# Three moves in a hybrid decoder block: B's bonus, down's first split, and the PSUM pool of one run of small matmuls

## The chip, the cores and the metric

The kernel runs on one core of a Trainium2 chip. The metric is the device time of one execution in microseconds (us). A core has a matmul engine (TensorE, PE in the profile, with its weight loads shown as PEld), a vector engine (VectorE, DVE), a scalar engine (ScalarE, ACT), GpSimd (POOL), and a queue engine that issues most transfers (SyncE, SP). Each engine takes its own instructions in a fixed order and waits on semaphores for the others. Matmuls write into PSUM, of which the kernel has eight banks of 128 x 512 float32; DVE and ACT read results out of there.

## What is computed

The reference is one layer of a hybrid decoder over 16 meta tokens and 1024 tokens, width 1024:

```python
h = h + 0.5 * swiglu(rmsnorm(h), w_gu, w_down)             # first feed-forward network
aq, ak, av, az, abeta, aalpha, bcols, ga, gb = split(rmsnorm(h) @ w_in)
o_a = gated DeltaNet in chunks (aq, ak, av, ...)            # branch A, 8 heads of 128
o_b = RWKV-7 time mixing (bcols, ...)                       # branch B, 16 heads of 64
h = h + (sigmoid(ga) * o_a + sigmoid(gb) * o_b) @ w_out
h = h + 0.5 * swiglu(rmsnorm(h), w_gu2, w_down2)            # second network
return rmsnorm(h)
```

Two pieces of it are touched directly. Branch B adds a **bonus** to its output: `sum(r * k * r_k) * v`, the sum going over the 64 channels of a head. And the first matmul of the second half of each network (`down`) needs the hidden activations as its right-hand side.

## The kernel before

All large products are float32 products made of three matmuls on split operands: an operand x is written as hi + lo, where hi is a rounded copy (one ACT copy) and lo = x - hi (one DVE subtraction). The function `split` (L155) issues both, so in the profile ACT L159 is always a "hi" and DVE L160 a "lo". A weight tile of 128 x 1024 is loaded by SP (`wraw`), split into `w[:, 0]` and `w[:, 1]`, and used by 24 matmuls of 512 columns (`mm3`, L261): per 128 rows of the weight one with hi and hi, one with hi of the weight and lo of the activation, one with lo of the weight. At most one weight tile is split ahead of the one in use (`AHEAD`, `loadw`).

The time falls into three stages: the first network (to about 740 us), the middle with both branches (to about 2340 us), and the second network.

**The networks.** `gate_up` goes through the gate and up weights in units of seven half-size products each. Its hidden rows go to HBM (`hid`) and come back as `hr`, three loads ahead (`Hidden.AHEAD`); `Hidden.put` splits a row into an `hd` tile. The generator `Hidden.ahead` is stepped by the last two units of `gate_up`: its stages issue, in this order, the first loads, then nothing, a weight fetch, the first split into the tile `hd0`, nothing, a weight fetch. `down` then multiplies the rows by the down weights (`pd` in the profile).

**The middle.** It runs 16 passes, one for each of eight column groups (j) and two segments of the sequence. The first eight passes have 528 columns (512 and the meta tokens), the last eight 512. Each pass is a list of actions, each a function, and the actions of neighbouring passes are interleaved by hand: `REGULAR` is "merge_blocks transitions operands+ inverses+ chains gates finish decay++ new_b++ new_a++", where one + means the next pass and two the one after. So the order of the text around the change is: `transitions` of a pass, `operands` of the next; and `new_b`, then `new_a` of the one after.

- `new_b` (L1138) makes three projections (v, k, r), then the normalised key `kkn` by a column sum (`cs`), then by some nine DVE operations the tiles AR and BK, and at its end the bonus: `bv = r * r_k * k` (L1181), a split of `bv` into `hl`, two matmuls with a block-diagonal matrix of ones (`bon`, through `colsum`, L1032), and the multiplication by v (L1186).
- `new_a` (L1189) makes three projections, each followed by a convolution of three taps on DVE (L1209), a sigmoid on ACT, and, for the first two, a column sum (`cs`) through the same `hl` tile, of which there is one.
- `operands` makes the products `grb` (evacuated into LT, L1250), `gra` (evacuated into UA and attn, L1290 and L1292), `bkt`, `vp` and others, all in banks of the pool `mx`. LT and UA go to HBM and come back as `Ub`, which is the input of `inverses`: 62 small DVE operations (L1400, L1402), whose result goes through HBM again to `merge_blocks`.
- `transitions` (L1464) makes a serial row of small products by `run` (L1085): `xp`, `xp` again, `vp`, `mp` and at last `np`, each in two banks. Results of `mp` are read by six DVE operations (mt, L1508, four times; AR, L1511, twice), those of `np` by five (vbk, L1514 and L1515; yb, L1517).
- `chains` is the recurrence itself, 4 steps for A and 8 for B, each a matmul and a DVE or ACT operation in turn, in banks of the pool `ch`. `finish` ends the pass. The last pass has the order `FINAL`: "gates merge_blocks transitions chains fill finish", with half of the output projection (`pwo`) as `fill`.

The eight PSUM banks of the middle: the pool `ch` has two. The pool `mm` for projections has two tiles of two banks, and `mx` two banks, up to the action `banks` in the seventh pass; from there `mm` has three tiles of one bank and `mx` three. The small rotating tiles of DVE and ACT (xr, acc, v, k, r and others) share eight buffers (`NTMP`).

The framework records the instructions in the order of the text, gives each tile its buffer and each engine its order and its waits. The orders are fixed when the program is built, by a plan that takes an instruction as soon as it holds it to be ready.

Of the kernel before, what the change touches and what calls it, by code (L numbers as in the profile page):

```python
# [9 lines left out]
F32R = mybir.dt.float32r  # L10
AF = mybir.ActivationFunctionType
ALU = mybir.AluOpType
# [14 lines left out]
FULL = 512  # L27
# [127 lines left out]
def split(g, src, hi, lo, eng=None, hi_eng=None):  # L155
    if hi_eng:
        hi_eng.tensor_copy(hi, src)
    else:
        g.nc.scalar.activation(hi, src, AF.Copy)  # L159
    (eng or g.nc.vector).tensor_tensor(lo, src, hi.bitcast(F32), op=ALU.subtract)  # L160
# [400 lines left out]
class Hidden:  # L561
# [20 lines left out]
    def ahead(self):  # L582
        for f in range(self.AHEAD):
            self.load(f)
        yield
        yield
        fetchw(self.g)
        yield
        self.first = self.put(self.tile(self.pool, F32R, "hd0", "hd0", 1, [2]))
        yield  # L590
        yield
        fetchw(self.g)
        yield
# [330 lines left out]
def proj(g, c, ct, full=False):  # L924

    w = loadw(g, "win", ct)
    lo, n = (c.off, FULL) if full else (0, c.n)
    ps = mm_tile(g, "pp", n, FULL // 2 + c.off)
    for c0, cn in halves(n, FULL // 2 + c.off):
        sl = slice(lo + c0, lo + c0 + cn)  # L930
        mm3(g, ps[:, c0 : c0 + cn], w, KD, lambda k: (c.u[k][:, 0, sl], c.u[k][:, 1, sl]))
    return ps
# [135 lines left out]
def run(g, pool, name, *kinds):  # L1068


    ps, out, used = {}, [], [0, 0]
    for f in kinds:
        ds = [f(i, 0)[2] ^ f(i, 0)[3] for i in range(2)]
        at = []
        for d in ds:
            if d not in ps:
                ps[d] = pool.tile([P, 512], F32, name=name, tag=pool.name)
            at.append(used[d])
            used[d] += NCB // 2 * CB
        for i in range(NCB):  # L1080
            e, c0 = ds[i & 1], at[i & 1] + i // 2 * CB
            for h in range(2):
                l, r, src, dst = f(i, h)
                assert src ^ dst == e
                g.nc.tensor.matmul(ps[e][HS[dst], c0 : c0 + CB], lhsT=l, rhs=r, start=True, stop=True)  # L1085
        out.append([(ch3(ps[d][:, c0 : c0 + NCB // 2 * CB], CB), cs) for d, c0, cs in zip(ds, at, EO)])
    return out
# [50 lines left out]
def new_b(g, q):  # L1138

    nc, st, V, c, j, n, off, it = g.nc, g.st, g.V, q.c, q.j, q.n, q.off, q.it  # L1140
    meta = q.s == 0
    fs = slice(off, off + FULL)
    tmp = lambda name, w=528: tmp_tile(g, name, w)
    EN, ELx, av, elm = q.EN, q.ELx, q.av, meta and q.elm

    v = shifted(g, c, 48 + j, 16 + j, "vB")


    Vs = q.Vs = st.tile([P, NCB, CB], F32, name="Vs", tag="Vs", bufs=2)
    k = shifted(g, c, 40 + j, 8 + j, "kB")  # L1150
    for ps, cs in run(g, g.mx, "vbp", lambda i, h: (v[HS[h], off + i * CB : off + (i + 1) * CB],
                                                    g.C("cmat")[HS[h], HS[h]], h, key(i, h)))[0]:
        nc.scalar.activation(Vs[:, cs], ps, AF.Copy)
    if meta:
        ps = g.mx.tile([P, 512], F32, name="vbm", tag="mx")
        nc.tensor.matmul(ps[:16, 0:P], lhsT=v[:, 0:16], rhs=g.C("cmat"), start=True, stop=True)
        nc.scalar.activation(g.uvm[it % 2][0:16, :], ps[:16, 0:P], AF.Copy)

    r = shifted(g, c, 32 + j, j, "rB")
    kkn = tmp("kkn")  # L1160
    colsum_rsqrt(g, "bd", k[:, :n], kkn, kkn, n, 1.0, V("eps"), pre=V("kk", j))
    nc.vector.scalar_tensor_tensor(kkn[:, :n], k[:, :n], V("kk", j), kkn[:, :n], op0=ALU.mult, op1=ALU.mult)
    t1 = tmp("t1")
    nc.vector.tensor_tensor(t1[:, :n], av[:, :n], kkn[:, :n], op=ALU.mult)
    nc.scalar.activation(av[:, :n], av[:, :n], AF.Identity, scale=V("ka", j), bias=V("oka", j))
    nc.vector.tensor_tensor(k[:, :n], k[:, :n], av[:, :n], op=ALU.mult)
    BK = q.BK = st.tile([P, NCB, 2, CB], F32, name="BK", tag="BK")
    nc.vector.tensor_tensor(BK[:, :, 1, :], ch3(k[:, fs], CB), ch3(EN[:, fs], CB), op=ALU.mult)
    nc.vector.scalar_tensor_tensor(BK[:, :, 0, :], ch3(t1[:, fs], CB), -1.0, ch3(EN[:, fs], CB),
                                   op0=ALU.mult, op1=ALU.mult)  # L1170
    AR = q.AR = st.tile([P, NCB, 2, CB], F32, name="AR", tag="AR", bufs=2)
    nc.vector.tensor_tensor(AR[:, :, 0, :], ch3(kkn[:, fs], CB), ELx[:, :, 0:CB], op=ALU.mult)
    if meta:
        arm = q.arm = st.tile([P, 16], F32, name="arm", tag="arm", bufs=2)
        nc.vector.tensor_tensor(arm, kkn[:, 0:16], elm[:, 0:16], op=ALU.mult)
        nc.vector.tensor_tensor(g.bkm[:, 0:16], k[:, 0:16], EN[:, 0:16], op=ALU.mult)
        nc.vector.scalar_tensor_tensor(g.bkm[:, 32:48], t1[:, 0:16], -1.0, EN[:, 0:16], op0=ALU.mult, op1=ALU.mult)

    nc.vector.tensor_tensor(AR[:, :, 1, :], ch3(r[:, fs], CB), ELx[:, :, 1:], op=ALU.mult)
    bv = q.bv = st.tile([P, FULL], F32, name="bv", tag="bv", bufs=2)  # L1180
    nc.vector.scalar_tensor_tensor(bv, r[:, fs], V("rk", j), k[:, fs], op0=ALU.mult, op1=ALU.mult)  # L1181
    ps = g.mx.tile([P, 512], F32, name="bon", tag="mx")
    hi, lo = parts_tile(g, FULL)
    split(g, bv, hi, lo)
    colsum(g, ps, "bd", hi, lo)
    nc.vector.tensor_tensor(bv, ps, v[:, fs], op=ALU.mult)  # L1186


def new_a(g, q):  # L1189

    nc, st, V, c, j, n, off = g.nc, g.st, g.V, q.c, q.j, q.n, q.off
    meta = q.s == 0
    tmp = lambda name, w=528: tmp_tile(g, name, w)
    kq = q.kq = st.tile([P, 2, 528], F32, name="kq", tag="kq", bufs=2)
    for wi, base in ((0, 8), (1, 0), (2, 16)):
        ct = base + j
        ps = proj(g, c, ct)
        xr = tmp("xr", 531)
        acc = tmp("acc")
        if c.s == 0:  # L1200
            nc.gpsimd.memset(xr[:, 0:3], 0.0)
        else:
            nc.gpsimd.tensor_copy(xr[:, 0:3], g.carA[:, ct, :])
        nc.scalar.activation(xr[:, 3 : 3 + n], ps, AF.Copy)
        nc.scalar.activation(acc[:, :n], ps, AF.Identity, scale=V("convw", ct * 4 + 3))  # L1205
        if c.s == 0:
            nc.gpsimd.tensor_copy(g.carA[:, ct, :], xr[:, n : n + 3])
        for tap in (2, 1, 0):
            nc.vector.scalar_tensor_tensor(acc[:, :n], xr[:, tap : tap + n], V("convw", ct * 4 + tap), acc[:, :n],  # L1209
                                           op0=ALU.mult, op1=ALU.add)  # L1210
        sg = xr
        sigm(nc, sg[:, :n], acc[:, :n], scale=-1.0)
        nc.vector.tensor_tensor(acc[:, :n], acc[:, :n], sg[:, :n], op=ALU.mult)
        if wi < 2:
            colsum_rsqrt(g, "ones", acc[:, :n], sg, sg, n, 1.0, V("eps"),
                         bias=V("lnq") if wi == 1 else None)
            nc.vector.tensor_tensor(kq[:, wi, :n], acc[:, :n], sg[:, :n], op=ALU.mult)
    Va = q.Va = st.tile([P, NCA, P], F32, name="Va", tag="Va", bufs=2)
    ps = g.mx.tile([P, 512], F32, name="vap", tag="mx")
    for i in range(NCA):  # L1220
        nc.tensor.transpose(ps[:, i * P : (i + 1) * P], acc[:, off + i * CA : off + (i + 1) * CA], g.C("ident"))
    nc.scalar.activation(Va, ch3(ps, P), AF.Copy)
    if meta:
        vkm = q.vkm = st.tile([16, 2, P], F32, name="vkm", tag="vkm", bufs=2)
        ps = g.mx.tile([P, 512], F32, name="vmp", tag="mx")
        nc.tensor.matmul(ps[:16, 0:P], lhsT=acc[:, 0:16], rhs=g.C("ident"), start=True, stop=True)
        nc.scalar.activation(vkm[:, 0, :], ps[:16, 0:P], AF.Copy)
# [236 lines left out]
def transitions(g, q):  # L1464

    nc, st = g.nc, g.st
# [3 lines left out]
    xa, xv = (st.tile([P, NCB, CB], F32, name=x, tag=x) for x in ("xa", "xv"))  # L1470
# [9 lines left out]
    def by_tok(l, r):  # L1480
        def f(i, h):
            t = tok(i, h)
            return l(HS[t], i), r(HS[t], i), t, h
        return f
# [18 lines left out]
    bt = lambda r, i: BKt[r, i, i & 1]  # L1503
    br = lambda r, i: LT[r, i, i & 1, CB:]
# [4 lines left out]
                                    op=ALU.add)  # L1509
    for ps, cs in pr:  # L1510
        nc.vector.tensor_tensor(AR[:, cs, 1, :], ps, AR[:, cs, 1, :], op=ALU.add)  # L1511
    pn, py = run(g, g.ch, "np", by_tok(bt, lambda r, i: xv[r, i]), by_tok(lambda r, i: xv[r, i], br))
    for ps, cs in pn:
        nc.vector.tensor_tensor(vbk[:, cs], ps, vbk[:, cs], op=ALU.add)  # L1514
    nc.vector.tensor_tensor(vbk, vbk, q.gam.unsqueeze(2).to_broadcast([P, NCB, CB]), op=ALU.mult)  # L1515
# [222 lines left out]
```

## Time and profile before

| | us |
|---|---|
| median of 3 runs | 3052.4 |
| the runs | 3052.31 to 3053.04 |
| the profiled execution: its own time | 3048.16 |
| its span, first to last instruction | 3046.4 |
| PE busy, first network and its down (0 to 740) | 725.67 of 740 |
| PE busy, the middle (740 to 2340) | 1524.02 of 1600 |
| PE busy, second network (2340 to 3046) | 692.58 of 706 |
| DVE busy in the same three | 392.91, 1226.64, 388.19 |

The profile comes from one execution of its own, 4.2 us faster than the median of the runs. Its page gives each engine's busy time; the trace behind it gives every instruction with its start, and for an idle stretch ahead of it the instruction that ended the stretch (written `[idle <- what ended it]`). A row of the timeline reads: start, duration (us), engine, line, operation, output <- inputs, shape, how many in a row. A row of the waits reads: who waited <- for whom: total us, times, the longest. A row of the windows reads: the stretch, its length, then the busy time of PE, PEld, DVE, ACT and POOL with the number of instructions, the granted clock of PE as a share, the share of the transfer engines, and GB/s.

### The profile page before, as it was taken

Reading aid. Unit: us, or ns where it says so; the run is one execution under the profiler, and the core shown is the slowest. Engines: PE = TensorE matmul, PEld = TensorE weight load, DVE = VectorE, ACT = ScalarE, POOL = GpSimd, SP = SyncE. Lnnn points to the kernel's source line nnn. Section 1 sums busy time; section 2 is a strip of 40 time slices with the busy share of each in tenths; the row PEclk is TensorE's granted clock in tenths of the full one; section 3 lists DMA queues with packets and bytes.
Section 4 is the critical chain, followed back from the end, with each engine's and each line's share of the span. In section 5 each row is a group of like instructions: output and inputs, shape, how many; then the busy total and the mean of one; then the engine's idle time right before and its main releaser. Section 6 shows DMA issues by size and latency. Waiting matters only on the chain.

```text
span 3046.4 us, 61663 instructions
## 1 busy us (share of the span) xinstructions
PE 2942.3 (97%) x25498; PEld 2530.1 (83%) x25498; DVE 2007.7 (66%) x3872; ACT 1372.2 (45%) x2404; POOL 348.6 (11%) x503
## 2 busy tenths in 40 slices
PE   8999999999989999999998999999999999999998
PEld 8999998998878888888776777777786888888886
DVE  7555554346668877778868888777766755556246
ACT  5322222125645656556565655665544432223114
POOL 0322220000000000000000110010000032232000
PEclk9999999999999999999999999999999999999999
DMA  3232224234222322233332333223345132225223
GB/s 127 83 98 84 83 82 160 81 94 149 80 67 72 78 74 67 78 82 97 82 92 67 91 80 81 74 74 88 106 145 178 64 104 90 83 83 202 58 80 115
DMA packets 257593, 287.19 MB, mean 94 GB/s; under 512 B 169296, under 2 KB 175440, under 8 KB 257312
## 3 DMA queue, kind: packets, MB, share of 16 engines
q1 hardware_dynamic: 253072, 271.43, 30.2%
q0 software_dynamic: 2512, 8.65, 0.8%
q8 instruction: 201, 3.29, 0.5%
q10 hardware_dynamic: 1728, 3.16, 0.3%
q14 instruction: 80, 0.66, 0.1%
HBM read 232.70 MB, written 50.47 MB: 93 GB/s over the span
## 4 chain that ended last, share of the span: by engine, by line
PE 52%; DVE 10%; ACT 5%; issue 2%; DMA 1%; SPq 0%; DVEq 0%; ACTq 0%
PE pp L261 16%; PE pg L448 13%; PE pd L261 8%; PE pwo L261 3%; PE pg L472 1%; DVE w L160 1%; DVE tb L1400 1%; DVE Xb L1402 1%; ACT w L159 1%; PE vp L1085 1%; PE cs L1032 1%; PE mp L1085 1%; PE np L1085 1%; DVE mt L1508 1%; PE bkt L1317 1%
## 5 line engine op out<-in xcount | busy, mean ns | idle before, releaser
L261 PE MATMUL pp<-uk,w 128*128 128x512 f32 (+2 forms) x4824 | 966.6, 346 | 9.3 <-DVE w L160 5.7
L261 PEld LDWEIGHTS pp<-uk,w 128*128 128x128 f32 x4824 | 741.3, 190 | 105.5 <-DVE w L160 13.2
L159 ACT ACTIVATE w<-wraw 128x1024 fp32r<-128x1024 f32 (+2 forms) x330 | 326.4, 989 | 497.5 <-PE pd L261 301.7
L261 PE MATMUL pd<-hd,w 128*128 128x512 f32 (+2 forms) x2448 | 454.4, 346 | 5.3 <-ACT hd L159 3.1
L160 DVE TENSOR_TENSOR w<-wraw,w 128x1024 fp32r<-128x1024 f32 (+2 forms) x330 | 403.2, 1222 | 74.8 <-ACT w L159 64.9
L261 PEld LDWEIGHTS pd<-hd,w 128*128 128x128 f32 x2448 | 391.8, 189 | 63.9 <-ACT hd L159 3.3
L448 PE MATMUL pg<-bt,w 128*128 128x256 f32 (+2 forms) x2520 | 400.7, 317 | 0.0
L448 PEld LDWEIGHTS pg<-bt,w 128*128 128x128 f32 x2520 | 360.4, 188 | 32.8
L454 DVE TENSOR_TENSOR c<-c,pg 128x520 f32<-128x520 f32 (+1 forms) x280 | 189.6, 689 | 278.3 <-PE pg L448 250.6
L448 PE MATMUL pg<-b,w 128*128 128x256 f32 (+2 forms) x2160 | 347.8, 317 | 0.0
L448 PEld LDWEIGHTS pg<-b,w 128*128 128x128 f32 x2160 | 309.8, 188 | 28.0
L159 ACT ACTIVATE w<-wrx 128x1024 fp32r<-128x1024 f32 (+1 forms) x64 | 58.4, 913 | 289.8 <-PE pg L448 247.9
L418 POOL TENSOR_TENSOR wrx<-wrx 128x512 f32<-128x512 f32 x38 | 52.5, 1382 | 732.8 <-DVE w22b L160 519.0
L1402 DVE TENSOR_TENSOR Xb<-Xb,tb 115x126 f32<-115x126 f32 (+22 forms) x496 | 125.4, 253 | 9.1 <-DVE tb L1400 0.4
L1400 DVE TENSOR_TENSOR tb<-Ub,Xb 115x126 f32<-115x126 f32 (+22 forms) x496 | 124.1, 250 | 8.1 <-DMA Ub<-scr 0.9
L1209 DVE SCALAR_TENSOR_TENSOR acc<-xr,pk,acc 128x528 f32<-128x528 f32 (+1 forms) x144 | 108.8, 756 | 28.6 <-ACT acc L1205 28.0
L624 DVE SCALAR_TENSOR_TENSOR h<-pd,h 128x528 f32<-128x528 f32 (+1 forms) x64 | 44.6, 698 | 116.4 <-PE pd L261 116.4
L624 DVE SCALAR_TENSOR_TENSOR hh<-pd,hh 128x512 f32<-128x512 f32 x64 | 44.1, 690 | 115.2 <-PE pd L261 115.2
L261 PE MATMUL pwo<-uk,w 128*128 128x512 f32 x384 | 99.7, 413 | 4.1 <-DVE w L160 1.9
L261 PEld LDWEIGHTS pwo<-uk,w 128*128 128x128 f32 x384 | 73.8, 197 | 21.9 <-ACT w L159 2.7
L160 DVE TENSOR_TENSOR w<-wrx,w 128x1024 fp32r<-128x1024 f32 (+1 forms) x64 | 66.6, 1041 | 14.9 <-ACT w L159 14.8
L159 ACT ACTIVATE hd<-hr 128x1040 fp32r<-128x1040 f32 (+1 forms) x40 | 41.2, 1061 | 63.3 <-DMA hr<-hid 38.3
(420 smaller groups left out, 4200.4 us busy)
## 6 DMA issues: line engine op xcount, KB each, us to landing
wraw<-in_win SPq DMA_DIRECT2D x150, 512.0 KB
wraw<-in_wgu SPq DMA_DIRECT2D x44, 512.0 KB
wrx<-in_wgu SPq DMA_DIRECT2D x44, 512.0 KB
wraw<-in_wdn SPq DMA_DIRECT2D x48, 320.0 KB
wraw<-in_wdn SPq DMA_DIRECT2D x32, 384.0 KB
hid<-c SPq DMA_DIRECT2D x44, 260.0 KB
hr<-hid SPq DMA_DIRECT2D x22, 520.0 KB
hid<-c SPq DMA_DIRECT2D x44, 256.0 KB
```

Of the source, the lines that this page charges most:

```text
L159: g.nc.scalar.activation(hi, src, AF.Copy)
L160: (eng or g.nc.vector).tensor_tensor(lo, src, hi.bitcast(F32), op=ALU.subtract)
L261: g.nc.tensor.matmul(ps, lhsT=l, rhs=r, start=i == 0, stop=i == n - 1)
L418: sums.tensor_tensor(a22, a21, a22, op=ALU.add)
L448: nc.tensor.matmul(ps[:, c0 : c0 + cn], lhsT=l[:, x, k, :], rhs=r[:, k, y, c0 : c0 + cn], start=i == 0, stop=i == 3 * HK - 1)
L454: nc.vector.tensor_tensor(o, x, y, op=ALU.add)
L472: nc.tensor.matmul(ps[:, c0 : c0 + cn], lhsT=l[:, x, k, :], rhs=r[:, k, y, c0 : c0 + cn], start=i == 0, stop=i == 6 * HK - 1)
L624: nc.vector.scalar_tensor_tensor(hv, pd, 0.5, hv, op0=ALU.mult, op1=ALU.add)
L1085: g.nc.tensor.matmul(ps[e][HS[dst], c0 : c0 + CB], lhsT=l, rhs=r, start=True, stop=True)
L1209: nc.vector.scalar_tensor_tensor(acc[:, :n], xr[:, tap : tap + n], V("convw", ct * 4 + tap), acc[:, :n], op0=ALU.mult, op1=ALU.add)
L1400: nc.vector.tensor_tensor(tv, U[:, i, i + 1 :].unsqueeze(2).to_broadcast([npt, nt, ncc]), X[:, i, 0:ncc].unsqueeze(1).to_broadcast([npt, n ...
L1402: nc.vector.tensor_tensor(X[:, i + 1 :, 0:ncc], X[:, i + 1 :, 0:ncc], tv, op=ALU.add)
```

## The change

Three places are edited; nothing is added to or taken from the computation.

1. In `Hidden.ahead` the split into `hd0` moves two stages of the generator ahead, from the last unit to the one before it.
2. The bonus leaves the end of `new_b` (only `bv` is made there) and becomes a function `bonus`, called in `new_a` behind the matmuls of the second projection (q), ahead of that projection's evacuation.
3. The last run of `transitions`, `np`, takes its two banks from the pool `mx` instead of `ch`.

```diff
@@ class Hidden, ahead() @@
             self.load(f)
         yield
+        self.first = self.put(self.tile(self.pool, F32R, "hd0", "hd0", 1, [2]))
         yield
         fetchw(self.g)
         yield
-        self.first = self.put(self.tile(self.pool, F32R, "hd0", "hd0", 1, [2]))
         yield
         yield
@@ new_b @@
     nc.vector.scalar_tensor_tensor(bv, r[:, fs], V("rk", j), k[:, fs], op0=ALU.mult, op1=ALU.mult)
+    q.v = v
+
+
+def bonus(g, q):
+
     ps = g.mx.tile([P, 512], F32, name="bon", tag="mx")
     hi, lo = parts_tile(g, FULL)
-    split(g, bv, hi, lo)
+    split(g, q.bv, hi, lo)
     colsum(g, ps, "bd", hi, lo)
-    nc.vector.tensor_tensor(bv, ps, v[:, fs], op=ALU.mult)
+    g.nc.vector.tensor_tensor(q.bv, ps, q.v[:, q.off : q.off + FULL], op=ALU.mult)
@@ new_a @@
         ps = proj(g, c, ct)
+        if wi == 1:
+            bonus(g, q)
         xr = tmp("xr", 531)
@@ transitions @@
-    pn, py = run(g, g.ch, "np", by_tok(bt, lambda r, i: xv[r, i]), by_tok(lambda r, i: xv[r, i], br))
+    pn, py = run(g, g.mx, "np", by_tok(bt, lambda r, i: xv[r, i]), by_tok(lambda r, i: xv[r, i], br))
```

## The prediction

> **What bounds the kernel now.** I read the page's busy shares first, then TensorE's waits, then the timeline around each wait.
>
> ```profile
> span 3046.4 us, 61663 instructions
> PE 2942.3 (97%) x25498; PEld 2530.1 (83%) x25498; DVE 2007.7 (66%) x3872; ACT 1372.2 (45%) x2404; POOL 348.6 (11%) x503
> PE bon L1032 <- ACT hl L159: 17.8, 13, 7.6
> ...
> PE np L1085 <- DVE AR L1511: 9.0, 14, 1.0
> ```
>
> TensorE (PE) is busy 97% of the span: 3046.4 - 2942.3 = 104 us are idle, and no edit here removes a matmul. So the change can win only from those 104 us. The wait rows (total us, times, longest) put two of the edits beside two waits: the bonus at 17.8, `np` at 9.0. Their sum, 26.8 us, and what down's first split may have, is the ceiling. A wait removed counts only if PE doesn't meet the same late engine a few matmuls on, so I look at what is late next in each place.
>
> Is VectorE (DVE) a second bound? A stretch of one regular pass of the second half, from the first row of the inverses to the bonus:
>
> ```profile
> 1942.00:1984.00 42.00, 40.40 (x244) 32.01 (x243) 39.47 (x107) 26.89 (x49) 6.22 (x11) 1.00 0.36 93
> ```
>
> The columns are PE, weight loads, DVE, ACT. In these 42 us DVE works 39.5, with no room, though over the span it works 66%. So each pass holds a loop: PE's `mp`, then DVE's evacuations up to UA, the copies to HBM and back, 40 us of full DVE, and PE again at the bonus. What lies on this loop sets the pass; a PE wait off it is only slack.
>
> **Edit 1, down's first split.** It removes and adds nothing: one ACT copy and one DVE subtraction change their place in the text. Where do they run now?
>
> ```profile
> 77.73 1.08 ACT L159 ACTIVATE hd<-hr 128x1040 fp32r<-128x1040 f32 x1
> 79.39 1.24 DVE L160 TENSOR_TENSOR hd<-hr,hd 128x1040 fp32r<-128x1040 f32 x1
> 2411.86 1.05 ACT L159 ACTIVATE hd<-hr 128x1024 fp32r<-128x1024 f32 x1
> 476.07 13.71 SPq L574 DMA_DIRECT2D hr<-hid  x6
> 483.75 0.86 PE L261 MATMUL pd<-hd,w 128*128 128x256 f32 x4 [3.10 <-ACT hd L159]
> ```
>
> The first split runs at 77.7 us, some 395 us before down uses it, and at 2411.9 in the second network, although the text has it in the last unit. Each engine's order is evidently fixed ahead, ready work being drawn forward; the text only says which of two ready instructions goes first. Moved by half a unit, the split still competes with the same early units. The wait of 3.10 us belongs to a later row, loaded at 476.07 once its buffer is free. No transfer moves with it, so no queue is passed: the load stays where it was. **Cost: 0.** If the split did move, it could cost its own 1.08 + 1.24 = 2.3 us in each network, or win at most the 3.1.
>
> **Edit 2, the bonus.** The same two matmuls, one ACT copy and two DVE operations in each of 16 passes, now behind the matmuls of A's second projection and, in precedence, behind A's first convolution. The waits of six regular passes run from 1722.85 to 2157.41; one of them in full:
>
> ```profile
> 1722.85 0.50 PE L1032 MATMUL bon<-hl,bdr 128*128 128x512 f32 x1 [1.47 <-ACT hl L159]
> ...
> 1973.50 8.80 PE L261 MATMUL pp<-uk,w 128*128 128x512 f32 x38
> 1983.79 0.50 PE L1032 MATMUL bon<-hl,bdr 128*128 128x512 f32 x1 [1.49 <-ACT hl L159]
> ...
> 1985.99 6.30 PE L261 MATMUL pp<-uk,w 128*128 128x512 f32 x27
> ...
> 2157.41 0.50 PE L1032 MATMUL bon<-hl,bdr 128*128 128x512 f32 x1 [1.31 <-ACT hl L159]
> 1983.11 0.63 ACT L159 ACTIVATE hl<-bv 128x512 fp32r<-128x512 f32 x1 [0.68 <-DVE bv L1181]
> 1984.92 0.68 DVE L160 TENSOR_TENSOR hl<-bv,hl 128x512 fp32r<-128x512 f32 x1
> 1985.52 0.74 DVE L1209 SCALAR_TENSOR_TENSOR acc<-xr,pk,acc 128x512 f32<-128x512 f32 x1
> ```
>
> A projection is 24 matmuls at 8.80/38 = 0.23 us. Of the 38, 24 are the first projection and 14 the second; so 10 of the second are left when PE stops for the ACT half of the split. With the bonus behind them PE runs these 10 from 1982.3 to 1984.6, the ACT half (ready at 1983.7) is there, and the first bonus matmul waits for nothing. **Late next** is the DVE half: it ends at 1985.6 now, and at about 1986.25 if the convolution's tap (0.74 us, the row behind it) now goes first. So PE still waits about 0.7 to 1.4 us, one matmul later. Of the 27 matmuls behind the second bonus matmul 24 are the third projection's, so today the second and both bonus matmuls are done at 1985.99 + 3 x 0.23 = 1986.7; then at 1985.8 to 1986.5. Gain 0.2 to 0.9; I take 0.5, as the new order of the two DVE rows isn't known. Six regular passes of the second half: 3.0 us. The other waits at the bonus make 17.8 - 7.6 (below) - 6 x 1.45 = 1.5 us, in six places of the first half: half, 0.7. The longest wait is different:
>
> ```profile
> 1623.53 0.74 PE L261 MATMUL pp<-uk,w 128*128 128x512 f32 x2 [0.42 <-ACT w L159]
> 1631.86 0.79 PE L1032 MATMUL bon<-hl,bdr 128*128 128x512 f32 x1 [7.60 <-ACT hl L159]
> 1632.48 1.22 PE L261 MATMUL pp<-uk,w 128*128 128x512 f32 x2
> 1631.22 1.22 DVE L160 TENSOR_TENSOR w<-wraw,w 128x1024 fp32r<-128x1024 f32 x1
> 1632.00:1634.00 2.00, 2.00 (x5) 1.33 (x6) 2.00 (x6) 0.00 (x0) 0.00 (x0) 0.50 0.29 35
> ```
>
> PE had done two matmuls of the second projection, which need only the high half of the weight; the third needs the low half, which DVE finishes at 1632.4. Without the bonus PE would wait there all the same: 0.3 us to win, not 7.6. Edit 2: 3.0 + 0.7 + 0.3 = **4.0 us gained** (between 0 and 10: 6 x 1.45 + 1.5 if nothing is late next). Nothing is queued behind the new wait but the projections; the multiplication of the bonus frees B's `v` buffer some 6 us later, and no wait of PE names what uses those eight rotating buffers next.
>
> The granted clock behind that 7.6 us gap is 0.50 in the two microseconds shown (third figure from the right), so 2 x 0.50 = 1 us of PE's pace was lost there. The Trainium skill, "TensorE: Matmul & The Clock Gate", section on the HAM clock gate, says that an idle stretch over some 3.4 us halves the clock until PE has been busy for about as long. The trace agrees; by that rule the gap's end would save this 1 us too, and the sum would be 9.0. I keep the gap, so it isn't in the sum.
>
> **Edit 3, `np` into the operands' banks.** It removes PE's wait for `ch`: its two banks are freed by six DVE operations behind `mp`. Count for count the work stays.
>
> ```profile
> 1923.33 0.66 ACT L1500 ACTIVATE xv<-xp 128x256 f32<-128x256 f32 x2 [1.17 <-PE xp L1085]
> 1926.32 1.73 DVE L1508 TENSOR_TENSOR mt<-mp,ck 64x256 f32<-64x256 f32 x4 [1.35 <-PE mp L1085]
> 1928.06 0.76 DVE L1511 TENSOR_TENSOR AR<-mp,AR 128x256 f32<-128x256 f32 x2
> 1928.63 0.95 PE L1085 MATMUL np<-xv,BKt 64*64 64x64 f32 x30 [0.77 <-DVE AR L1511]
> 1930.04 1.56 PE L1286 MATMUL gra<-kq 128*128 128x256 f32 x6
> ...
> 1933.44 0.41 DVE L1292 TENSOR_TENSOR attn<-gra,E 128x256 f32<-128x256 f32 x1
> 1926.00:1934.00 8.00, 7.23 (x170) 5.63 (x162) 7.51 (x21) 0.60 (x1) 0.00 (x0) 1.00 0.11 16
> ```
>
> `np` will run at once behind `mp`, as xv is ready (1923.33). But it then holds two of the two (first half) or three (second) operands' banks until DVE has done eleven operations instead of six, and the second set of `grb`, then `gra`, queue for them. The wait moves from `np` to `grb`. For the loop: from 1926.32 to 1933.85 DVE works 7.5 of 7.5 us (the window row), and has the same operations to do in another order; UA, and with it the copies, come out at the same time if PE feeds it. So of the 9.0 us I count a quarter, **2.5 us** (between +9.0, all, and -20, below). Cover for PE meanwhile are the gates' projections (72 matmuls a pass).
>
> In the last pass no operands follow, so only the gain stays:
>
> ```profile
> 2269.20 2.37 PE L261 MATMUL pwo<-uk,w 128*128 128x512 f32 x9
> 2271.55 0.86 PE L1085 MATMUL np<-xv,BKt 64*64 64x64 f32 x27
> 2275.02 0.46 PE L1558 MATMUL p<-SA,kq 128*128 128x128 f32 x2 [0.40 <-PE pwo L261]
> 2301.70 1.73 PE L1032 MATMUL cs<-hl,bdr 128*128 128x512 f32 x2 [2.82 <-ACT hl L1046]
> 2304.21 2.08 PE L261 MATMUL pwo<-uk,w 128*128 128x512 f32 x4 [0.78 <-ACT rg L1051]
> ```
>
> `np` could start at 2269.2 instead of 2271.55, the serial chain behind it about as much sooner, and at its end PE idles 2.82 + 0.78 = 3.6 us for want of the chain. I take **1.5 us**, since ACT's other splits also stand ahead there (0 to 3.6).
>
> **Sum.** 0 + 4.0 + 2.5 + 1.5 = 8.0 us from the profiled execution's 3048.16 (span 3046.4 and 1.8 around it): 3040.2. The runs' median, 3052.4, lies 4.2 above that execution, so 3044.4.
>
> **Rivals.**
> - *All listed waits go.* For it: each is PE standing at one named wait. Against it: the DVE half of the split and the low weight are seen to end later. Of 17.8, 7.3 stay with the weight; 10.5 + 9.0 + 1.5 = 21 us: 3031. The Trainium skill, "Perfetto Trace Analysis", Optimization Strategy, reads equal gaps that repeat as a sign of too few PSUM buffers; by that rule `np`'s whole 9.0 would go here, 6.5 more than in my sum. The trace agrees with the sign (9.0 us in 14 passes), but not with the remedy as far as it takes the banks from `grb`. Chance 0.12.
> - *Nothing changes:* the loop through DVE sets every pass, PE meets it one wait later. For it: the full 42 us of DVE. Against it: in the first half PE's waits are short and spread. 3052. Chance 0.26.
> - *Slower: the operands starve.* Place: from `np` to UA in 14 passes. `grb` (about 0.5 us) and `gra` (1.56/6 x 4 = 1.0) were hidden behind DVE's work on `mp` and `np`; with the banks held they fall between DVE's last `yb` and LT, UA, and DVE stands still. Price 1.5 us x 14 = 20, on the loop, with only the bonus's 4.0 against it: 3052.4 + 20 - 4 = 3068. It decides once UA ends more than (8 + 6)/14 = 1.0 us later behind `mp` than today's 7.5. Chance 0.17.
>
> **How the numbers follow.** Forecast 0.45, rivals 0.12, 0.26, 0.17. A measurement tells about 0.2%, 6.1 us, from no change. The forecast case spreads from 3 to 13 us gained, two thirds of it over 6.1: 0.30 faster, 0.15 same. Faster 0.30 + 0.12 = 0.42; same 0.15 + 0.26 = 0.41; slower 0.17. The range 3029 to 3060 takes in the first two rivals and the near half of the third.
>
> **What would show it.** Edit 1: the first split still near 78 and 2412 us. Edit 2: `bon` waits on hl's DVE half for about 1 us in passes 9 and up, the total below 12 us with one wait near 7 us left on w or `bon`. Edit 3: `np` without a wait, `grb` or `gra` with one on yb; UA's end 7.5 us behind `mp`; the wait of 2.82 at 2301 nearly gone. I am wrong if the engines' orders change elsewhere (a first pass that waits longer for weights), or if DVE's full stretch moves as a whole.

## The result, and the profile after

| | us |
|---|---|
| before, median of 4 runs | 3052.36 (3050.68 to 3053.04) |
| after, median of 4 runs | 3086.3 (3084.08 to 3090.21) |
| ratio after / before | 1.0114, 95% interval 1.0102 to 1.0126 |
| profiled execution after: its own time, span | 3085.94, 3084.2 |

The change makes the kernel 34 us slower. The prediction was 3044.4 us with a range of 3029 to 3060; it gave "slower" 0.17.

The page's span and busy shares after:

```profile
span 3084.2 us, 61657 instructions
PE 2970.9 (96%) x25498; PEld 2549.3 (83%) x25498; DVE 1989.6 (65%) x3872; ACT 1382.7 (45%) x2404; POOL 325.7 (11%) x503
```

and TensorE's waits after (who waited <- for whom: total us, times, longest):

```profile
PE pp L261 <- DVE w L160: 28.6, 19, 4.1
PE iv L1442 <- DMA Xc<-scX: 10.7, 7, 1.8
...
PE np L1085 <- ACT xv L1507: 2.7, 14, 0.2
```

Both waits at which the change aimed are gone: `bon` had 17.8 us and is no longer in the list, `np` had 9.0 for AR and has 2.7 for xv. In their place stand the projections' wait for the low half of a weight (5.7 before, 28.6 now), and a wait for Xc (2.9 before, 10.7 now), the input that the inverses send back through HBM. In all, PE's idle time went from 104 to 113 us, and its busy time grew by 28.6, although it does the same matmuls. Part of that is the clock: the mean granted clock of the profiled execution is 0.993 before and 0.990 after, by estimate 0.003 x 3084 = 9 us.

Where is the time? The start of `mp`'s evacuation (DVE `mt`) marks a pass, and the time to the next such start is called its period. The first period is 80.8 us before and 97.9 after; from the third to the seventh pass it is 94.0 before and 95.8 to 99.0 after; in passes 10 to 14 some 87 in both. The first six periods together lose 38 us, the seventh wins 4 (129.6 and 125.7), and the eighth and ninth lose 7. So the loss lies in the first pass and in the first half. One pass there, the fifth, before: evacuation of `mp`, of `grb` (LT), end of UA and attn, first and last DVE row of the inverses, `iv`, the next pass.

```profile
1263.80 1.73 DVE L1508 TENSOR_TENSOR mt<-mp,ck 64x256 f32<-64x256 f32 x4 [2.27 <-PE mp L1085]
1266.21 1.28 DVE L1250 TENSOR_TENSOR LT<-grb,ck 128x512 f32<-128x512 f32 x2
1273.88 0.42 DVE L1292 TENSOR_TENSOR attn<-gra,E 128x256 f32<-128x256 f32 x1
1286.29 0.18 DVE L1400 TENSOR_TENSOR tb<-Ub,Xb 115x31 f32<-115x31 f32 x1
1318.13 0.62 DVE L1403 COPY Yt<-Xb 115x512 f32<-115x512 f32 x1
1336.96 0.25 PE L1435 MATMUL iv<-Xc,LT 32*32 32x32 f32 x2
1357.85 1.73 DVE L1508 TENSOR_TENSOR mt<-mp,ck 64x256 f32<-64x256 f32 x4 [2.27 <-PE mp L1085]
```

The same places after, with the last evacuation of `np` (yb) and the start of `grb`:

```profile
1293.55 1.73 DVE L1515 TENSOR_TENSOR mt<-mp,ck 64x256 f32<-64x256 f32 x4 [5.08 <-PE mp L1085]
1297.56 0.42 DVE L1524 TENSOR_TENSOR yb<-np,yb 128x256 f32<-128x256 f32 x1
1298.00 1.58 PE L1254 MATMUL grb<-AR,BK 64*64 64x128 f32 x32
1307.21 0.41 DVE L1299 TENSOR_TENSOR attn<-gra,E 128x256 f32<-128x256 f32 x1
1318.60 0.19 DVE L1407 TENSOR_TENSOR tb<-Ub,Xb 115x31 f32<-115x31 f32 x1
1361.04 0.63 DVE L1410 COPY Yt<-Xb 115x512 f32<-115x512 f32 x1
1372.49 0.74 PE L1442 MATMUL iv<-Xc,LT 32*32 32x32 f32 x32 [1.38 <-DMA Xc<-scX]
1389.32 1.73 DVE L1515 TENSOR_TENSOR mt<-mp,ck 64x256 f32<-64x256 f32 x4 [5.09 <-PE mp L1085]
```

Counted from `mt`, attn ends at 10.5 us before and 14.1 after. That is the quantity that the prediction named as deciding, and it is 3.6 us later. `grb` starts at 1298.00, when yb ends (1297.56 + 0.42), 4.5 us behind `mt`; before, its first rows ran from 1257.7, 6 us ahead of `mt`, and LT came 2.4 us behind `mt`, ahead of `np`'s evacuations. DVE doesn't stand still meanwhile: up to the end of attn it is busy 9.0 of 10.5 us before and 12.2 of 14.1 after, because 3.2 us of other work (a weight's low half, the chain, the gates) now run ahead of UA. The inverses start 2.6 us later, and their last row, Yt, 13.2 us later (54.3 and 67.5). PE, which met Xc without a wait, now waits for it.

In passes 10 to 14 Yt is some 10 us later too (59 to 60 us behind `mt`, 49 before), but there PE still comes to Xc without a wait, and the period hardly moves.

In the first pass the shift is larger. These are the last attn of the second pass's operands and the first `mt`, before:

```profile
895.46 0.40 DVE L1292 TENSOR_TENSOR attn<-gra,E 128x256 f32<-128x256 f32 x1
901.39 1.73 DVE L1508 TENSOR_TENSOR mt<-mp,ck 64x256 f32<-64x256 f32 x4 [3.83 <-PE mp L1085]
```

and after:

```profile
900.24 1.73 DVE L1515 TENSOR_TENSOR mt<-mp,ck 64x256 f32<-64x256 f32 x4 [6.46 <-PE mp L1085]
913.61 0.41 DVE L1299 TENSOR_TENSOR attn<-gra,E 128x256 f32<-128x256 f32 x1
```

Before, all of these operands were done 5.5 us ahead of `mp`'s evacuation; after, they end 13.8 us behind it.

### The profile page after: what moved, and what is told of

It reads as the page before. It is cut to its first block, busy times and chain, and to the rows that moved or that the text cites. A ratio compares the mean times of both kernels' runs of the same rounds, so it can differ in the third digit from the quotient of the medians.

```text
span 3084.2 us, 61657 instructions
## 1 busy us (share of the span) xinstructions
PE 2970.9 (96%) x25498; PEld 2549.3 (83%) x25498; DVE 1989.6 (65%) x3872; ACT 1382.7 (45%) x2404; POOL 325.7 (11%) x503
## 4 chain that ended last, share of the span: by engine, by line
PE 76%; DVE 14%; ACT 4%; issue 3%; DMA 2%; SPq 1%; DVEq 0%; ACTq 0%
PE pg L448 25%; PE pd L261 15%; PE pp L261 15%; PE pg L472 3%; PE pwo L261 2%; DVE w L160 2%; DVE Xb L1409 2%; DVE tb L1407 2%; PE xp L1085 1%; DMA Xc<-scX 1%; DVE acc L1216 1%; PE grb L1254 1%; PE vp L1085 1%; PE cs L1032 1%; PE mp L1085 1%
## 5 line engine op out<-in xcount | busy, mean ns | idle before, releaser
L261 PE MATMUL pp<-uk,w 128*128 128x512 f32 (+2 forms) x4824 | 984.4, 347 | 34.8 <-DVE w L160 28.6
L261 PEld LDWEIGHTS pp<-uk,w 128*128 128x128 f32 x4824 | 751.3, 190 | 135.8 <-DVE w L160 36.1
L160 DVE TENSOR_TENSOR w<-wraw,w 128x1024 fp32r<-128x1024 f32 (+2 forms) x330 | 402.9, 1221 | 89.1 <-ACT w L159 81.9
L1515 DVE TENSOR_TENSOR mt<-mp,ck 64x256 f32<-64x256 f32 x64 | 27.0, 422 | 72.4 <-PE mp L1085 71.8
```

Source lines behind the costliest of these rows:

```text
L261: g.nc.tensor.matmul(ps, lhsT=l, rhs=r, start=i == 0, stop=i == n - 1)
```

## The experiments

Each experiment is compared with executions of the kernel before that were taken beside it. Their medians are 3049.0 to 3049.7 us, about 3 below the 3052.4 above, so the ratios say more than the times.

**Theory 1** (edit 3): a bank of a pool goes from tile to tile in the order of the text. `np` now takes two banks of `mx` ahead of the next pass's `grb`, so `grb`, LT, `gra` and UA must all stand behind `np` and its evacuation; before, part of them, and in the first pass all, ran ahead of it. In the first half `mx` has two banks, so all of `grb` waits; from the seventh pass it has three, and a part of `grb` finds a bank free. **Theory 2** (edit 2): the bonus's new place lets other DVE work pass the split of the weights.

### Each edit alone

`e1_np_only` is the kernel before with this line alone:

```diff
-    pn, py = run(g, g.ch, "np", ...
+    pn, py = run(g, g.mx, "np", ...
```

> The kernel before with edit 3 alone (np in the operands' banks in all 16 passes). Theory 1 (edit 3 costs: the next pass's grb must follow np in the row of banks, so LT and UA come later behind mp, by 19 us in the first pass and 3 to 5 in passes 2 to 7, and with them the inverses of the next pass): the whole loss is here, 3078 to 3095 us, UA's end some 14 us behind mp in passes 3 to 7. Theory 2 (the bonus's new place costs: PE waits for the weight's low half behind DVE's taps): about 3045 to 3053 us here, UA near 10.5 us behind mp.

Measured 3083.84 us (3079.11 to 3088.76), ratio 1.0111 (1.0096 to 1.0126): the whole loss of the three edits together. The fifth pass of its timeline:

```profile
1289.82 1.73 DVE L1508 TENSOR_TENSOR mt<-mp,ck 64x256 f32<-64x256 f32 x4 [5.65 <-PE mp L1085]
1303.90 0.41 DVE L1292 TENSOR_TENSOR attn<-gra,E 128x256 f32<-128x256 f32 x1
1360.58 0.62 DVE L1403 COPY Yt<-Xb 115x512 f32<-115x512 f32 x1
1371.94 0.74 PE L1435 MATMUL iv<-Xc,LT 32*32 32x32 f32 x32 [0.51 <-DMA Xc<-scX]
1388.65 1.73 DVE L1508 TENSOR_TENSOR mt<-mp,ck 64x256 f32<-64x256 f32 x4 [5.65 <-PE mp L1085]
```

attn ends 14.5 us behind `mt`, 4.0 later than before; Yt starts at 70.8 instead of 54.3, and the period is 98.8 instead of 94.0. How do 4.0 us become 4.8 when two waits, `xp`'s and `np`'s, are gone? A stretch of the third pass of this kernel by windows (PE, weight loads, DVE, ACT, POOL, then the granted clock):

```profile
1154.00:1156.00 2.00, 0.24 (x2) 0.02 (x1) 2.00 (x4) 1.97 (x4) 1.30 (x1) 1.00 0.00 0
1156.00:1158.00 2.00, 1.86 (x10) 1.86 (x11) 1.91 (x7) 1.88 (x3) 0.28 (x1) 0.66 0.35 82
1158.00:1160.00 2.00, 2.00 (x11) 2.00 (x11) 2.00 (x5) 1.31 (x3) 0.00 (x0) 0.50 0.44 180
```

and the row of the timeline that ends PE's idle time in it:

```profile
1156.14 5.38 PE L261 MATMUL pp<-uk,w 128*128 128x272 f32 x29 [1.90 <-DVE w L160]
```

The late inverses run in the time in which DVE also has the convolutions' taps and the splits of the weights: DVE is at 2.00 of 2.00, and PE waits 1.90 us for the low half of a weight. Behind that gap the clock is 0.66 and 0.50 for two windows: 2 x 0.34 + 2 x 0.50 = 1.7 us more. In the fifth pass PE's idle time grows by 0.9 us (3.2 to 4.1) and its busy time by 3.9; 1.7 of these are the clock, and most of the rest, by the estimate below, is a loss of cover. These rows group the projections in the chain's stretch (18.9 us before, 19.4 in `e1_np_only`). Before:

```profile
L261 PE MATMUL pp<-uk,w 128*128 128x512 f32 x26 | 8.2, 423 | 0.0
L261 PE MATMUL pp<-uk,w 128*128 128x272 f32 x10 | 1.7, 298 | 0.0
```

and in `e1_np_only`:

```profile
L261 PE MATMUL pp<-uk,w 128*128 128x272 f32 x28 | 5.8, 312 | 0.0
L261 PE MATMUL pp<-uk,w 128*128 128x256 f32 x24 | 5.0, 305 | 0.0
```

The wide matmuls of the gates, which filled the chain, are used up while PE would wait for Xc, and narrow ones fill the chain: 52 of them in 10.8 us, 0.21 us each between the chain's steps, where 57 in a row took 7.07 us (0.124 each) before. With 0.23 for a wide matmul (four of `gat` stand beside the 26 before) and 0.124 for a narrow one, this is 8.1 us of work before and 6.4 in `e1_np_only`, in a stretch 0.5 us longer: some 2 us.

`e2_bonus_only` is edit 2 alone (the diff is that of the change).

> The kernel before with edit 2 alone (the bonus behind A's second projection). Theory 1: 3042 to 3053 us, the bonus's waits of 17.8 us gone, in part replaced by waits for a weight's low half; UA's end as before (10.5 us behind mp in passes 3 to 7). Theory 2: 3072 to 3090 us, with waits of pp for DVE's low half of the weight of 20 us or more.

Measured 3055.43 us (3054.01 to 3063.09), ratio 1.0019 (1.0009 to 1.0029). Theory 2 falls as the cause of the 34 us, but theory 1's "not slower" falls too: edit 2 alone costs 6 us. The first period is 89.6 us (80.8), but most of these 8.8 are the granted clock, at 0.50 from 906 to 918 us and from 954 to 960 in this execution, whose time is 7.7 us over the median. Passes 3 to 6 take 93.4 to 93.5 (94.0 to 94.1), passes 10 to 14 88.5 to 90.2 (86.9 to 87.2). In the timeline of pass 11 the bonus waits for nothing, and PE waits some 6 us behind its second matmul:

```profile
1926.25 0.38 ACT L1463 ACTIVATE T<-iv 64x256 f32<-64x256 f32 x1
1926.68 0.50 PE L1466 MATMUL iv<-Y,T 64*64 64x64 f32 x5 [1.93 <-ACT T L1463]
1935.29 1.73 DVE L1515 TENSOR_TENSOR mt<-mp,ck 64x256 f32<-64x256 f32 x4 [1.92 <-PE mp L1085]
1943.38 0.41 DVE L1299 TENSOR_TENSOR attn<-gra,E 128x256 f32<-128x256 f32 x1
1637.09 3.35 PE L261 MATMUL pp<-uk,w 128*128 128x512 f32 x7 [8.22 <-DVE w L160]
```

The 1.49 us at the bonus have become 1.93 at the inverses' copy T, and attn ends 8.5 us behind `mt` instead of 7.5. The last row is the long gap, in the eighth period: without the bonus PE stands there for the weight's low half, 8.22 us.

### Where in the passes

`e3_np_last_pass`, `e4_np_second_half` and `e11_np_first_pass` put `np` into `mx` in some passes only:

```diff
-    pn, py = run(g, g.ch, "np", ...
+    pn, py = run(g, g.mx if q.it == 2 * NJ - 1 else g.ch, "np", ...   # e3
+    pn, py = run(g, g.mx if q.it >= NJ else g.ch, "np", ...           # e4
+    pn, py = run(g, g.mx if q.it == 0 else g.ch, "np", ...            # e11
```

> The kernel before with np in the operands' banks in the last pass alone, where no operands follow. Theory 1 and the prediction's own term: 1 to 3 us faster than before, 3049 to 3051.5 us, with the stretch from the last mp to the end of the middle shorter by that. Rival (another ACT split ends last there): no change, 3052.4.

Measured 1.0002 (0.9993 to 1.0011): no win that the runs resolve, though 1.5 us lie within the interval. The bulk of `np` starts 1.5 us after the first of `mp` (4.1 before) and the chain's last step comes 1.6 us sooner, but the wait behind it doesn't move:

```profile
2303.29 0.63 PE L1032 MATMUL cs<-hl,onesr 128*128 128x512 f32 x2
2306.73 0.54 PE L1032 MATMUL cs<-hl,bdr 128*128 128x512 f32 x1 [2.82 <-ACT hl L1046]
```

It is 2.82 us as before, and its row comes 32.4 us behind the last `mt`, 32.5 before. The first `cs` stands behind 42 matmuls of the output projection that PE does after the chain (35 before), and the second waits for ACT's work on the first. That is a link of its own, which the earlier chain didn't shorten.

> The kernel before with np in the operands' banks in passes 9 to 16 alone, where these are three banks. Theory 1 (what counts is how much later UA ends behind mp, and there it was 1.5 us in the changed kernel): up to 7 x 1.5 = 10 us lost less np's wait of 0.7 a pass, 3050 to 3060 us. Rival (with three banks nothing is held up and np's wait is won): 3044 to 3050 us.

Measured 1.0007 (0.9997 to 1.0016), no change that the runs resolve: attn ends 9.1 us behind `mt` instead of 7.5 in passes 10 to 14, and the periods are 87.0 to 87.3 us, as before. In the second half a delay of 1.5 us costs nothing, and the wins bring nothing: PE idles 0.7 to 0.9 us less a pass, but is busy that much longer.

> The kernel before with np in the operands' banks in the first pass alone. If the start is a loss of its own (LT and UA of the second pass, 5.5 us ahead of mp before, come some 13 us behind it): the first period is 93 to 98 us in place of 80.8 and the later ones are as before, 3060 to 3067 us. Rival (the start catches up: later passes run shorter until the old rhythm is back): 3050 to 3056 us.

Measured 3055.07 us, 1.0021 (1.0012 to 1.0031). The first period is 93.9 us, 13.1 more; but the total is only 6 us up, as the second (91.6 for 93.5), seventh (126.3 for 129.6) and ninth (82.7 for 86.4) are shorter, while the eighth is longer (89.2 for 84.6). So about half of the start's loss is caught up. In `e1_np_only`, where `np` is moved in every pass, it wasn't: passes 2 to 6 each lost 3.7 to 5.3 us more. Passes 2 to 8 weren't run by themselves; by difference from these runs they carry most of the 34 us.

### The suspected cost by itself, and the other way round

`e5_banks_held` leaves `np` in `ch` and adds two tiles that hold the operands' banks:

```diff
+    if q.it < 2 * NJ - 1:
...
+        for x in range(2):
+            ps = g.mx.tile([P, 512], F32, name="hd", tag="mx")
+            nc.tensor.matmul(ps[HS[0], :16], lhsT=AR[HS[0], x, 1, :], rhs=xv[HS[0], x, :16], ...)
+            nc.vector.tensor_copy(hold[HS[0], x], ps[HS[0], :16])
     pn, py = run(g, g.ch, "np", ...
```

> The kernel before, np left in ch, with the suspected cost alone added: behind mp two tiles are taken from the operands' banks in the row ahead of the next pass's grb, each with one small matmul that reads AR as mp's evacuation leaves it and one small copy by DVE (passes 1 to 15; the copies go nowhere). Theory 1 (grb has to stand behind mp's evacuation in the row of banks): grb, LT and UA move behind mp in the first pass (as with edit 3, some 12 us there), and UA ends 1 to 4 us later behind mp in passes 3 to 7 with 1.2 times that in each pass's period: 3062 to 3085 us. Rival (what costs is np's own new place, early beside mp, and the chain behind it): 3049 to 3058 us, the 60 small instructions themselves being at most 8 us.

Measured 3104.37 us, 1.0184 (1.0167 to 1.02): the rival falls as the whole cause, and the loss is larger than theory 1 had it. The first period is 100.0 us (80.8), and the first six together lose 30 us, where `e1_np_only` loses 36: holding the operands' banks is enough for most of the loss there. attn ends 14.5 us behind `mt` in pass 5, as in `e1_np_only`. In passes 9 to 15 it ends at 11.1 to 13.1, and the periods of passes 9 to 14 grow from 87 to 89 to 92. There the added tiles hold the operands back longer than `np` does (9.1 in `e4_np_second_half`, at no cost), so that part of the loss says nothing of edit 3. The price of a late UA is no fixed multiple: in the fifth pass 4.0 us cost 1.8 here and 4.8 in `e1_np_only`. With the same attn, Yt starts 64.9 us behind `mt` here and 70.8 there; why DVE's order differs so stays open. `np` in `mx` but behind the operands would have taken away the forced order alone; it wasn't tried.

`e9_operands_ahead_of_np` and `e10_operands_ahead_of_all` move the operands ahead in the text (`np` in `ch`; in the first, `np` and its evacuations are an action of their own, `late_np`):

```diff
-REGULAR = "merge_blocks transitions operands+ inverses+ ..."
+REGULAR = "merge_blocks transitions operands+ late_np inverses+ ..."   # e9
+REGULAR = "merge_blocks operands+ transitions inverses+ ..."           # e10
```

> The kernel before with np (left in ch) and its five evacuations behind the next pass's operands in the text: LT, UA come directly behind AR's evacuation. Theory 1 read the other way (UA's end behind mp starts the inverses and sets the pass): UA ends 2 to 3 us sooner behind mp (near 5 in passes 9 and up, near 8 in passes 3 to 7), the periods shrink by 1 to 3 us, 3025 to 3045 us. Rival (the chain, whose first steps need np's vbk and yb, then sets the pass, or PE's own 84 us of work does): 3048 to 3065 us.

> The kernel before with the next pass's operands ahead of the whole run of transitions in the text: LT and UA come before mp. Theory 1 the other way: UA ends 1 us or more before mp's evacuation starts, and the periods shrink further, by 2 to 3 us a pass down to PE's own work, 3015 to 3040 us. Rival (the time that UA wins mp and the chain lose, for they stand behind the operands on PE and DVE): 3050 to 3070 us.

Measured 3067.1 us (1.0057, 1.0042 to 1.0072) and 3053.19 (1.001, 1.0001 to 1.002). The periods of passes 10 to 14 are 87.5 to 88.0 us with attn 5.4 behind `mt`, and 86.3 to 88.4 with attn ahead of it. Neither is faster, so theory 1 falls where it is read the other way round, and the rivals are right in direction; the first is 17 us slower, 2 us beyond its rival's range, with 95.5 us in passes 3 to 6 and 135.8 in the seventh. The eleventh pass of the second of them:

```profile
1844.37 0.41 DVE L1292 TENSOR_TENSOR attn<-gra,E 128x256 f32<-128x256 f32 x1
1857.12 1.72 DVE L1508 TENSOR_TENSOR mt<-mp,ck 64x256 f32<-64x256 f32 x4
1895.51 0.61 DVE L1403 COPY Yt<-Xb 115x512 f32<-115x512 f32 x1
1944.27 1.72 DVE L1508 TENSOR_TENSOR mt<-mp,ck 64x256 f32<-64x256 f32 x4
```

attn ends 12 us ahead of `mt`, the inverses are done 38 us behind it instead of 49, and the pass still takes 87.2 us, with PE busy for 84.3 of them (84.1 of 86.9 before). So UA's time looks one-sided: sooner wins nothing, as PE's own work and its other waits then set the pass; later costs in the first half, where the inverses slide under other DVE work and PE then meets Xc with a wait. Both runs also put other work behind the operands, so that a small win isn't excluded.

### The bonus elsewhere

`e6` and `e7` put the bonus behind A's first or third projection (`if wi == 0`, `if wi == 2`), `e8` keeps the second but only for passes 3 to 8 (`if wi == 1 and 2 <= q.it < NJ`), `e12` mixes:

```diff
+    if q.it < 2:
+        bonus(g, q)                                  # old place, end of new_b
...
+        if q.it >= 2 and wi == 1 + q.it // NJ:       # in new_a
+            bonus(g, q)
```

> Edit 2 alone, but the bonus behind the matmuls of A's first projection in place of the second. Theory B1 (behind the second projection the bonus's ACT copy comes in ACT's full stretch and pushes ACT's copy T of the inverses' products, for which PE then waits 1.93 us in passes 10 and up): one projection earlier ACT has a gap of 3 us, T is not pushed, the period of passes 10 to 14 is at most 87 us, 3043 to 3051 us in all. Rival B2 (any place behind the first matmuls of A makes grb's first set fall behind xp, LT and UA 1 us later): period near 88.5 us, 3052 to 3058 us.

> Edit 2 alone, but the bonus behind the matmuls of A's third projection. Theory B1: the ACT copy falls still nearer to T and xp's copies, a wait of 1 us or more remains at T or xp in passes 10 to 14, period 88 us or more, 3053 to 3064 us. Rival B2 gives the same here as for the second projection, 3055 us.

> Edit 2 alone, and only for passes 3 to 8, whose periods were 93.4 us with it in place of 94.0; the first two passes and the second half keep the old place. If the gain of 0.6 us a pass is edit 2's own: 5 x 0.6 = 3 us faster than before, 0.9985 to 0.9995. Rival (it was won from the lateness of the first pass, which is gone here): no change.

Measured 0.9995 (0.9986 to 1.0004), 0.999 (0.9981 to 0.9999) and 0.9998 (0.9989 to 1.0007). Behind the first projection B1's forecast nearly holds (86.7 to 87.5 us in passes 10 to 14, with the bonus's wait of 1.5 us back), behind the third it fails (86.3 to 86.9, no wait for T): a fixed rule "the later, the worse" isn't what happens, and B2 falls in both. What decides seems to be where the plan then puts its neighbours. No place brings a regular pass of the second half below 86.3 us, whichever wait it removes. The third place costs 1.0 to 1.2 us in each of passes 3 to 5 (95.1 to 95.3 us) and wins 3.2 and 3.1 in the seventh and ninth periods. In passes 3 to 6 the second place takes 93.4 us also when nothing else is moved (`e8`), but 0.6 us a pass isn't resolved in the total.

> The bonus in its old place for passes 1 and 2, behind A's second projection for passes 3 to 8, behind the third for passes 9 to 16; no other edit. If the places add up pass by pass: 5 x 0.6 us from passes 3 to 7, 3.2 + 3.2 + 1.5 us from the periods of passes 7, 9 and 15, about 8 to 11 us faster than before, 0.9965 to 0.9975. Rival (a gain in one pass is met again in another): 0.999 to 1.000.

Measured 3038.22 us (3037.25 to 3039.39), 0.9964 (0.995 to 0.9977): faster than both kernels. The gains are in the passes where the single runs had them, but not of the same sizes: 93.1 to 93.6 us in passes 2 to 6, 128.5 in the seventh (1.1 won in place of 3.2), 81.1 in the ninth (5.2 in place of 3.2), 80.3 in the fifteenth (81.9); the eighth loses 1.8 (86.4). That the sum came out near the forecast is in part luck.

## Why the prediction was wrong

- **Edit 1: right, as far as the traces show.** It wasn't run by itself. The order of the work stayed, and so did the wait for a later row (3.10 before); the second network's first split comes at 2449.7 us, later by no more than the middle's delay:

```profile
77.91 1.08 ACT L159 ACTIVATE hd<-hr 128x1040 fp32r<-128x1040 f32 x1 [0.22 <-DMA hr<-hid]
483.82 6.42 PE L261 MATMUL pd<-hd,w 128*128 128x256 f32 x32 [2.97 <-ACT hd L159]
```

- **Edit 3 in the loops: the step that failed.** DVE "has the same operations to do in another order; UA, and with it the copies, come out at the same time if PE feeds it": PE can't feed it, since `grb` may not start until `np` is evacuated (4.5 us behind `mt` in the fifth pass), and DVE then doesn't have the same operations ahead of UA but 3.2 us more. The forecast, 2.5 us won, is 34 us lost in `e1_np_only`, beyond the bound of 20. The third rival had the right place and the right test (UA more than 1.0 us later), and the price wrong. It was read from one pass of the second half. There UA is indeed 1.5 us later, but partly by luck: DVE, which was to stand still, is busy 9.0 of 9.1 us (LT's first evacuation now comes behind `mp`), and `e4_np_second_half` shows no cost. In the first half, with two banks, the delay is 4.0 us, and in the first pass 19. And the rival took a late UA at its own length; in the first half it also moves the inverses under other DVE work. (A reading beside it: the row shown has DVE at 7.51 of 8.00 us; in the 7.53 us from `mt` to attn it is 7.35.)
- **Edit 3 in the last pass: sized wrong.** Forecast 1.5 us; `e3_np_last_pass` resolves no win, and the 2.82 us stay, for they belong to the two column sums.
- **Edit 2: the wait goes, as forecast, and the gain doesn't come.** The long gap stays on the weight's low half, as the prediction had it (8.22 us alone, 4.13 after). In the first half the gain is 0.6 us a regular pass, more than the 0.7 in all. But "late next" was looked for only at the bonus's own DVE half. In the changed kernel both matmuls of the bonus come without a wait, and the projection ahead of them has one:

```profile
1933.22 5.28 PE L261 MATMUL pp<-uk,w 128*128 128x512 f32 x22 [1.36 <-DVE w L160]
1941.21 0.39 PE L1032 MATMUL bon<-hl,bdr 128*128 128x512 f32 x1
1942.19 0.50 PE L1032 MATMUL bon<-hl,bdr 128*128 128x512 f32 x1
```

  Three taps of the convolution now stand ahead of the weight's low half on DVE. With edit 2 alone it is T instead. Forecast -4.0, measured +6 alone; beside edit 3 nothing of it is left to be seen (1.0114 and 1.0111).
- **The loop.** The prediction held that what lies on the loop through UA sets the pass. Half of that is right: later costs in the first half (`e1_np_only`, `e5_banks_held`), sooner wins nothing (`e10_operands_ahead_of_all`), and in the second half 1.5 us are free (`e4_np_second_half`).
- **The gap that repeats.** The Trainium skill, "Perfetto Trace Analysis", Optimization Strategy, says that an equal gap that repeats can mean that there isn't enough SBUF or PSUM for the next tile. Other banks did remove `np`'s wait of 9.0 us, and the kernel lost 34.

## What to carry to other kernels

Moving a tile to another pool moves it in that pool's row: list who takes the banks next, and look whether that work runs ahead of the mover today, in the first pass and in each half and not only in the pass that you happened to read. A wait removed on a saturated engine is worth little until it is clear what the engine does in the next twenty microseconds; price the delay of what now stands behind by the work that it then meets.

## What the runs showed of the hardware

The clock of PE fell without a long gap. In the changed kernel's first pass, by windows:

```profile
922.00:924.00 2.00, 1.38 (x9) 1.17 (x9) 1.06 (x5) 1.76 (x5) 0.00 (x0) 1.00 0.00 0
924.00:926.00 2.00, 1.34 (x8) 0.99 (x9) 1.35 (x6) 1.95 (x6) 0.00 (x0) 1.00 0.00 0
926.00:928.00 2.00, 1.12 (x8) 0.84 (x7) 2.00 (x7) 1.79 (x4) 0.39 (x1) 0.96 0.00 0
928.00:930.00 2.00, 1.86 (x12) 1.44 (x12) 1.32 (x6) 1.91 (x6) 0.19 (x1) 0.50 0.00 0
...
936.00:938.00 2.00, 2.00 (x10) 1.79 (x9) 1.19 (x6) 0.70 (x2) 0.20 (x1) 0.50 0.19 31
```

PE was busy 56 to 69% of three windows, with no wait over 0.9 us, and then ran ten microseconds at half the clock, so by estimate 5 us were lost. In `e1_np_only` one gap of 1.90 us was enough (the windows shown there). The gaps of 1.49 us at the bonus before were not: the granted clock is 1.00 over the whole twelfth pass. So a stall of PE is sometimes paid twice. The mean granted clock is about 0.992 in the runs of the kernel before and 0.986 to 0.989 in those of `e1_np_only`; by estimate 9 to 18 of its 34 us are the clock.

The Trainium skill, "TensorE: Matmul & The Clock Gate", section on the HAM clock gate, has the clock halved after an idle window of some 3.4 us. Here less was enough: the longest wait was 0.9 us in the one case, and the gap was 1.90 us in the other.
